# Block sums of the MLP's weights by adding transfers, and the MLP's pool opened ahead of the output projection

## The chip, the cores and the metric

The kernel runs on one core of a Trainium2 chip. The metric is device time in microseconds (us); before the change it was 2313.75 us, the median of three runs (2308.81 to 2314.91).

## The reference, cut to what matters

One residual block over 1024 tokens of width 1024, in float32:

```python
h = rms_norm(x, norm_mix_g)
q, k, v, conv_in, q_m, gate = split(h @ w_in)          # w_in: 1024 x 10240
y_attn = (diff_attention(q, k, v) normed) @ w_attn_o   # 8 heads, causal
y_conv = short_gated_conv(conv_in) @ w_conv_o
y_mem  = memory_attention(q_m, rms_norm(mem)) @ w_mem_o
merged = g0 * y_attn + g1 * y_conv + g2 * y_mem        # g = sigmoid(gate + b_gate)
x  = x + merged @ w_o                                  # the output projection
h2 = rms_norm(x, norm_mlp_g)
x  = x + relu(h2 @ w_mlp_in) ** 2 @ w_mlp_out          # the MLP, 1024 -> 4096 -> 1024
```

## The kernel before, in words

Every float32 matrix is split into a high part (a cast to fp32r on ACT) and a low part (raw minus high, on DVE or POOL), and every product is three matmuls: high by high, high by low, low by high. TensorE (PE) executes its instructions in the order in which the code issues them; the loads on the SP queue are pinned to one order too. DVE, ACT and POOL instructions are placed by a scheduler that respects the data and the buffers.

The program has five stages. (1) 0 to about 232 us: norm of x, keys, values and queries of the memory attention. (2) To about 1243 us: a loop of 64 attention passes (`for s in range(ns)`, L844 to L867; 8 heads by 8 row tiles). Between the steps of a pass, PE takes matmuls from a `stream` of independent products (conv inputs, gates). (3) The merge, to 1531.6 us: for the branches b = 2, 1, 0 (`branch_steps`), 8 column blocks each of the branch's output product. DVE multiplies it by its gate, POOL adds it to `merged`. In b = 0, ACT and DVE split `merged` at once into the tiles mT. (4) The output projection, to 1631.4 us: `w_o` in three column chunks (384, 384, 256), for each chunk 8 row tiles; 576 matmuls, 384 of them 384 wide, 192 of them 256 wide. DVE adds x, ACT squares, and in the last chunk `x2_norm(t)` scales the row tile (L885) and POOL issues its stores to `xn_dram` and `x2_dram`. (5) The MLP, in a new memory pool `xp`, whose tiles stand where the old pool's stood.

The MLP multiplies matrices of 2x2 blocks with seven block products (Strassen-Winograd) in place of eight. The up stage (`seq1`, `up(n)`) has 56 products of 24 matmuls each (8 column groups g by 7 products i), the down stage (`seq2`) 56 of 24 again. Four of the seven products need sums of weight blocks and four need sums of blocks of the normed rows. The weight sums are made by `sum_jobs` (w_mlp_in; 32 jobs: two SP loads of 256 KB into a tile `sumw`, four POOL operations of 128x256, one store of 512 KB issued by POOL), of which eight run in the attention loop (at `s % 8 == 6`) and the rest in the merge, and by `sum_jobs2` (w_mlp_out; 32 like jobs in the up stage). The rows come back from `xn_dram` into tiles `xr` (`load_rows`). `first_half(t)` transposes row tiles 0 to 3 on PE into X1 and X2 (`tps`, `put`: ACT casts the high part, DVE subtracts the low part). `second_sums(t)` makes the sums of rows t-4 and t (three POOL and one DVE subtraction into tiles tt and tu), and `second_half(t)` transposes them in three groups into X3 to X7, one t after each of the products up(0) to up(3). PSUM has two double banks named X and two named Z, which the transposes and the products share.

Of the kernel before, what the change touches and what calls it, by code (L numbers as in the profile page):

```python
# [60 lines left out]
def tile_hybrid_block(ctx: ExitStack, tc: tile.TileContext, x, mem, norm_mix_g, norm_mem_g, w_in, b_gate,  # L61
# [107 lines left out]

    def rstd_of(ss, n, width, tag):  # L170
# [3 lines left out]
        G.tensor_tensor(out=r, in0=r, in1=mhalf[:, 0:width], op=ALU.pow)  # L174
        return r
# [114 lines left out]
    sw1_dram = dram.tile([NG, P, 4, 4, 256], F32, name="sw1_dram")  # L290
    sw2_dram = dram.tile([NG, P, 4, 2, 512], F32, name="sw2_dram")
# [235 lines left out]
    def sub_(out, a, b):  # L527
        G.tensor_tensor(out=out, in0=a, in1=b, op=ALU.subtract)  # L528

    def sum_jobs():  # L530

        w1b = w_mlp_in.rearrange("(h k p) (c g n) -> h k p c g n", h=2, k=4, p=P, c=2, n=256)
        for g in range(NG):
            for k in range(4):
                z = rawt("sumw", (P, 2, 2, 256))
                for h in range(2):
                    load(z[:, h], w1b[h, k, :, :, g, :])
                a11, a21, a12, a22 = z[:, 0, 0], z[:, 0, 1], z[:, 1, 0], z[:, 1, 1]
                G.tensor_tensor(out=a22, in0=a21, in1=a22, op=ALU.add)  # L539
                sub_(a21, a11, a21)  # L540
                sub_(a11, a22, a11)
                sub_(a12, a12, a11)

                G.dma_start(sw1_dram[g, :, :, k, :], z.rearrange("p a b n -> p (a b) n"))
                yield

    def sum_jobs2(tile):
        w2b = w_mlp_out.rearrange("(h g j p) (d m n) -> h g j p d m n", h=2, j=2, p=P, d=2, n=256)
        for g in range(NG):
            for j in range(2):  # L550
                for m in range(2):
                    z = tile().rearrange("p a (b n) -> p a b n", b=2)
                    for h in range(2):
                        load(z[:, h], w2b[h, g, j, :, :, m, :])
                    b11, b12, b21, b22 = z[:, 0, 0], z[:, 0, 1], z[:, 1, 0], z[:, 1, 1]
                    sub_(b11, b12, b11)
                    sub_(b12, b22, b12)
                    sub_(b22, b22, b11)
                    sub_(b21, b21, b22)

                    G.dma_start(sw2_dram[g, :, :, j, m * 256:(m + 1) * 256], z.rearrange("p a b n -> p (a b) n"))
                    yield
# [4 lines left out]
    mT = ByChan()  # L567
# [23 lines left out]
    wos = [(0, 384, "wh"), (384, 384, "s"), (768, 256, "wh")]  # L591

    def load_wo(j):
        return load_w(w_o[:, wos[j][0]:wos[j][0] + wos[j][1]], wos[j][1], wos[j][2], V if j == 0 else None)

    def branch_steps(b):
        w_src = srcs[b][0]
        w, z = ready.pop(b)
        for c in range(KT):
# [3 lines left out]
            wn = load_w(w_src[:, (c + 1) * P:(c + 2) * P], P, "wh", V) if c + 1 < KT else None  # L603
            if b == 2:
                merged[c] = slot("merged", F32, tag="m")
            if c == KT - 1:
                if b:
                    prep(b - 1)
                else:
                    ready["wo"] = load_wo(0)  # L610
            if b == 0:
                mh, ml = mT.add("mT", ("fw" if c < 4 else "s", "m" if c else "s"))
            for hf in range(2):
# [3 lines left out]
                if hf:  # L617
                    run(jobs, 1)
# [221 lines left out]
    for s in range(ns):  # L840
# [24 lines left out]
        if s % 8 == 6:  # L865
# [348 lines left out]
```

## Time and profile before

The profiled execution took 2315.68 us; its span on the core is 2313.9 us.

| part of the span | us | PE busy | granted TensorE clock |
|---|---|---|---|
| whole | 2313.9 | 96% | 0.985 |
| attention loop, 300 to 1240 | 940.0 | 98% | 1.00 |
| merge, 1243 to 1531.6 | 288.6 | 97% | 0.98 |
| output projection, 1531.6 to 1631.4 | 99.8 | 94% | 0.95 |
| first MLP part, 1631.4 to 1740 | 108.6 | 70% | 0.81 |
| up stage, 1740 to 1940 | 200.0 | 100% | 1.00 |

Over the span DVE is busy 52%, ACT 41%, POOL 35%. PE's busy time is summed from records whose ends are modelled, so that a long row of matmuls is best timed by the starts of its first and last. A wait in a list names the engine or transfer whose end released the waiting instruction. A chain of waits goes backwards from the last instruction to what released it.

### The profile page before, as it was taken

Reading aid. Unit: us, or ns where it says so; the run is one execution under the profiler, and the core shown is the slowest. Engines: PE = TensorE matmul, PEld = TensorE weight load, DVE = VectorE, ACT = ScalarE, POOL = GpSimd, SP = SyncE. Lnnn points to the kernel's source line nnn. Section 1 sums busy time; section 2 is a strip of 40 time slices with the busy share of each in tenths; the row PEclk is TensorE's granted clock in tenths of the full one; section 3 lists DMA queues with packets and bytes.
Section 4 is the critical chain, followed back from the end, with each engine's and each line's share of the span. In section 5 each row is a group of like instructions: output and inputs, shape, how many; then the busy total and the mean of one; then the engine's idle time right before and its main releaser. Section 6 shows DMA issues by size and latency. Waiting matters only on the chain.

```text
span 2313.9 us, 31608 instructions
## 1 busy us (share of the span) xinstructions
PE 2219.8 (96%) x11472; PEld 1919.3 (83%) x11472; DVE 1213.6 (52%) x2200; ACT 953.1 (41%) x2190; POOL 811.6 (35%) x1084
## 2 busy tenths in 40 slices
PE   6999999999999999999999999989679999999999
PEld 6999888888888888888887887879568888788887
DVE  6755455555555555555556343342447676664452
ACT  5544445454545454444545232331222323354341
POOL 5422233333233232333334444641417788100000
PEclk9999999999999999999999999999789999999999
DMA  7412121222212121222214775752828999886660
GB/s 201 128 61 63 46 79 59 67 80 66 72 51 91 42 87 42 75 63 67 80 64 143 238 238 174 226 157 90 294 83 307 331 338 350 292 304 219 219 227 37
DMA packets 242748, 338.29 MB, mean 146 GB/s; under 512 B 20256, under 2 KB 182048, under 8 KB 242592
## 3 DMA queue, kind: packets, MB, share of 16 engines
q1 hardware_dynamic: 206128, 239.64, 32.5%
q0 software_dynamic: 19584, 71.31, 8.2%
q10 hardware_dynamic: 16880, 25.33, 3.1%
q8 instruction: 90, 1.47, 0.3%
q14 instruction: 66, 0.54, 0.1%
HBM read 235.56 MB, written 100.66 MB: 145 GB/s over the span
## 4 chain that ended last, share of the span: by engine, by line
PE 74%; DMA 10%; DVE 6%; POOL 4%; issue 3%; ACT 2%; SPq 1%; ACTq 0%; POOLq 0%; DVEq 0%
PE ps_mm L89 37%; PE X L89 14%; PE Z L89 11%; PE ps_sc L89 7%; DMA sumw<-in_w_mlp_in_dram 3%; PE ps_tr L93 3%; PE ps_tr L89 3%; POOL sumw L528 2%; DVE wlo L184 1%; DMA raw<-in_w_attn_o_dram 1%; DMA xr<-xn_dram 1%; SPq L98 1%; POOL merged L623 1%; DMA sw_dram<-sumw 1%; POOL sumw L539 1%
## 5 line engine op out<-in xcount | busy, mean ns | idle before, releaser
L89 PE MATMUL ps_mm<-hT,whi 128*128 128x512 f32 x1536 | 490.3, 400 | 1.7 <-DVE vst L668 1.7
L89 PEld LDWEIGHTS ps_mm<-hT,whi 128*128 128x128 f32 x1536 | 279.0, 189 | 53.3 <-DVE vst L668 4.7
L89 PE MATMUL ps_mm<-hT,wlo 128*128 128x512 f32 x768 | 301.7, 393 | 0.0
L89 PE MATMUL ps_mm<-whh,hT 128*128 128x384 f32 x1024 | 276.4, 340 | 1.9 <-DVE inner L475 1.9
L528 POOL TENSOR_TENSOR sumw<-sumw 128x256 f32<-128x256 f32 x224 | 215.0, 961 | 40.5 <-DMA sumw<-in_w_mlp_out_dram 29.6
L89 PEld LDWEIGHTS ps_mm<-whh,hT 128*128 128x128 f32 x1024 | 186.3, 188 | 7.2 <-DVE inner L475 3.7
L184 DVE TENSOR_TENSOR wlo<-raw,whi 128x256 fp32r<-128x256 f32 (+2 forms) x169 | 123.9, 749 | 121.4 <-ACT whi L202 108.6
L89 PE MATMUL X<-w,u 128*128 128x512 f32 x768 | 174.6, 389 | 0.0
L184 POOL TENSOR_TENSOR wlo<-raw,whi 128x512 fp32r<-128x512 f32 (+2 forms) x95 | 116.3, 1230 | 162.9 <-ACT whi L202 161.9
L89 PE MATMUL ps_mm<-whl,hT 128*128 128x384 f32 x512 | 171.4, 335 | 0.0
L89 PEld LDWEIGHTS X<-w,u 128*128 128x128 f32 x768 | 144.2, 188 | 29.9
L670 POOL TENSOR_TENSOR sq<-qk 128x256 f32<-128x256 f32 x64 | 42.6, 665 | 356.9 <-ACT qk L665 356.5
L89 PEld LDWEIGHTS ps_mm<-hT,wlo 128*128 128x128 f32 x768 | 144.7, 188 | 27.5
L202 ACT CAST whi<-raw 128x512 fp32r<-128x512 f32 (+2 forms) x264 | 127.0, 530 | 77.5 <-PE ps_mm L89 13.1
L174 POOL TENSOR_TENSOR r<-r,mhalf 128x1 f32<-128x1 f32 (+1 forms) x186 | 132.8, 714 | 14.4
L914 DVE TENSOR_TENSOR u<-uraw,u 128x1024 fp32r<-128x1024 f32 x56 | 72.1, 1288 | 118.9 <-ACT u L920 118.5
L89 PE MATMUL Z<-w,u 128*128 128x512 f32 x576 | 131.7, 390 | 1.6 <-DVE snap L917 1.6
L173 POOL TENSOR_SCALAR r<-ss 128x1 f32<-128x1 f32 (+1 forms) x186 | 39.7, 214 | 255.2 <-ACT ps_tr L764 106.0
L89 PEld LDWEIGHTS Z<-w,u 128*128 128x128 f32 x576 | 108.0, 188 | 24.8 <-DVE snap L917 2.4
L89 PE MATMUL ps_mm<-x,whi 128*128 128x512 f32 x384 | 120.6, 395 | 4.0 <-DVE x L184 3.3
L920 ACT CAST u<-uraw 128x1024 fp32r<-128x1024 f32 x56 | 59.0, 1054 | 156.9 <-PE X L89 74.6
L89 PE MATMUL ps_sc<-x,whi 128*128 128x512 f32 x384 | 118.8, 391 | 1.1 <-DVE gt L622 1.1
(236 smaller groups left out, 4836.1 us busy)
## 6 DMA issues: line engine op xcount, KB each, us to landing
sw_dram<-sumw POOLq DMA_DIRECT2D x64, 512.0 KB, 5.8
raw<-in_w_in_dram SPq DMA_DIRECT2D x56, 512.0 KB, 3.8
u_dram<-c POOLq DMA_DIRECT2D x56, 512.0 KB, 6.0
uraw<-u_dram SPq DMA_DIRECT2D x56, 512.0 KB, 5.3
sumw<-in_w_mlp_in_dram SPq DMA_DIRECT2D x64, 256.0 KB, 4.1
w1raw<-sw_dram SPq DMA_DIRECT2D x32, 512.0 KB, 6.6
sumw<-in_w_mlp_out_dram SPq DMA_DIRECT2D x64, 256.0 KB, 6.0
w2raw<-sw_dram SPq DMA_DIRECT2D x32, 512.0 KB, 4.3
```

The source lines that it names most:

```text
L89: return cls.pin(nc.tensor.matmul(*a, **kw))
L93: return cls.pin(nc.tensor.transpose(*a, **kw))
L98: return pin_load(nc.sync.dma_start(dst, src))
L173: G.tensor_scalar(r, ss, 1.0 / n, EPS, op0=ALU.mult, op1=ALU.add)
L174: G.tensor_tensor(out=r, in0=r, in1=mhalf[:, 0:width], op=ALU.pow)
L184: eng.tensor_tensor(out=lo, in0=raw, in1=f(hi), op=ALU.subtract)
L202: A.copy(out=hi[:, a:b, :], in_=raw[:, k0 + a:k0 + b, :])
L528: G.tensor_tensor(out=out, in0=a, in1=b, op=ALU.subtract)
L539: G.tensor_tensor(out=a22, in0=a21, in1=a22, op=ALU.add)
L670: G.tensor_tensor(out=sq, in0=qk, in1=qk, op=ALU.mult)
L914: eng.tensor_tensor(out=out, in0=a, in1=b, op=ALU.subtract)
L920: A.copy(out=hl[:, 0], in_=raw)
```

## The change

**Weight sums.** `sum_jobs` now issues 16 transfers from DRAM to DRAM on POOL's queue, eight for each weight, each of a quarter of a weight matrix (4.19 MB): eight plain copies and eight that add the source to what lies at the destination. A transfer that reads another one's result waits for it on POOL. One is issued at every third attention pass (`s % 3 == 1`, s = 1 to 46), behind the pass's last power operation of a norm. `sum_jobs2` and the `sumw` tiles are gone. Since the transfers only add, four operands have the opposite sign from before: `put` negates X4 and X5, and outputs are subtracted where they were added or squared after a minimum instead of a maximum. The loads of the sums read rows of 1 KB or 2 KB from the quarter matrices where they read one packed block.

**Merge and output projection.** In b = 0, POOL stores each half of `merged` to `mg_dram` (16 stores of 256 KB); the tiles mT are gone from the old pool. `old.close()` now stands ahead of the output projection. In the new pool, `load_m` brings `merged` back in pairs of column blocks and splits it, `load_wo` brings 8 full rows of blocks of w_o (512 KB) and splits them, `load_x` brings rows of x. The product is made in 512-wide halves, 384 matmuls in all: for t = 0 to 3 in four double banks at once, the column blocks k outside, 0 to 5 for all four, then the last two for each; then t = 4 to 7 one after the other.

**Rows of the MLP.** `wo_out` leaves the normed rows in SBUF (tiles xn, 7 buffers for 8 tiles); `xn_dram` is gone. `first_half(t - 4)` stands between the two halves of output tile t, `second_sums(t)` behind it, and the three groups of transposes of `second_half` stand between the matmuls of up(0) to up(3), eight matmuls apart. `seq1` begins with a list of 16 products. Some tiles change their pool slots (sn 4 to 3, c 6 to 7, halves for t, x's slots for the down stage's x2).

The diff, cut to its core:

```diff
+        last_norm[0] = G.tensor_tensor(out=r, in0=r, in1=mhalf[:, 0:width], op=ALU.pow)
...
+        def go(out, in_, op=ALU.bypass):
+            after(G.dma_start(out, in_, accum_op=op), last_norm[0])
+        a = [w_mlp_in[h * 512:(h + 1) * 512, c * 2048:(c + 1) * 2048] for c in range(2) for h in range(2)]
+        b = [w_mlp_out[h * 2048:(h + 1) * 2048, d * 512:(d + 1) * 512] for h in range(2) for d in range(2)]
+        for (q, t, r, s), z in ((a, sw1), ((b[0], b[2], b[1], b[3]), sw2)):
+            for i, src, op in ((0, r, 0), (1, r, 0), (0, s, 1), (1, q if z is sw1 else s, 1), (2, z[0 if z is sw1 else 1], 0),
+                               (2, q, 1), (3, z[2], 0), (3, t, 1)):
+                if z is sw2 and (i, op) == (0, 1):
+                    src = q
+                go(z[i], src, ALU.add if op else ALU.bypass)
                 yield
...
-            if b == 0:
-                mh, ml = mT.add("mT", ("fw" if c < 4 else "s", "m" if c else "s"))
...
-                    A.copy(out=mh[:, sl], in_=merged[c][:, sl])
-                    V.tensor_tensor(out=ml[:, sl], in0=merged[c][:, sl], in1=f(mh)[:, sl], op=ALU.subtract)
+                    G.dma_start(mg_dram[c][:, sl], merged[c][:, sl])
...
-        if s % 8 == 6:
+        if s % 3 == 1:
...
+    wo_op = [x8(f"wo{k}", (2, 1024)) for k in range(KT)]
+    m_op = {}
+    xn = {t: blk("xn", "c") for t in range(NT)}
+    m_op[1] = [x8("mT1", (2, 2, 512)) for _ in range(2)] + [wpair("mT1", 512) for _ in range(2)]
+    m_op[0] = [x8("mT0", (2, 2, 512)) for _ in range(4)]
+    tq = {t: half_blk("t2") for t in range(4, NT)}
+    xr = {}
+    def load_m(hf, kk):
+        r = raw4("mraw", 512)
+        load(r, mg_dram[2 * kk:2 * kk + 2, :, hf * 512:(hf + 1) * 512].rearrange("k p n -> p k n"))
+        split(m_op[hf][kk], r, V)
+    def load_wo(k):
+        r = raw4("woraw", 1024)
+        load(r, w_o[k * P:(k + 1) * P, :].rearrange("p (o n) -> p o n", o=1))
+        split(wo_op[k], r[:, 0, :], V)
+    def load_x(t):
+        xr[t] = blk("xr", "sn").rearrange("p h n -> p (h n)")
+        load(xr[t], x[t * P:(t + 1) * P, :])
...
+    def wo_out(t, ps):
+        x2 = xr.pop(t)
+        V.tensor_tensor(out=x2, in0=ps.rearrange("p h n -> p (h n)"), in1=x2, op=ALU.add)
+        ss = sm.tile([P, 1], F32, tag="ss1", bufs=3, name="ss")
+        xf = xn[t].rearrange("p h n -> p (h n)")
+        A.activation(xf, x2, AF.Square, accum_out=ss)
+        r = rstd_of(ss, D, 1, "r1")
+        V.scalar_tensor_tensor(out=xf, in0=x2, scalar=r, in1=g2_row, op0=ALU.mult, op1=ALU.mult)
+        G.dma_start(x2_dram[t], x2)
...
+    seq1 = [(0, 1), (0, 2), (1, 1), (1, 2), (0, 6), (0, 5), (0, 7), (1, 6), (0, 4), (1, 5), (0, 3), (1, 7), (2, 1),
+            (1, 4), (2, 2), (1, 3)]
...
-                load(r, sw1_dram[g, :, {6: 0, 7: 1, 3: 2, 5: 3}[i]])
+                load(r, sw1[{5: 0, 7: 1, 6: 2, 3: 3}[i]].rearrange("(k p) (g n) -> g p k n", p=P, n=256)[g])
...
+        if i in (4, 5):
+            A.activation(hi, src, AF.Copy, scale=-1.0)
+            V.scalar_tensor_tensor(out=lo, in0=src, scalar=-1.0, in1=f(hi), op0=ALU.mult, op1=ALU.subtract)
+        else:
+            A.copy(out=hi, in_=src)
+            sub(V, lo, src, f(hi))
...
+        ra, rb, n2 = xn[t - 4], xn[t], tq[t]
+        sub(G, ra[:, 0], rb[:, 0], ra[:, 0])
+        sub(V, rb[:, 0], rb[:, 1], rb[:, 0])
+        sub(G, n2, ra[:, 0], rb[:, 1])
+        add(G, ra[:, 1], ra[:, 1], n2)
...
+        ra, rb, n2 = xn.pop(t - 4), xn.pop(t), tq.pop(t)
+        for (i, a), (j, b) in (((3, rb[:, 1]), (7, rb[:, 0])), ((6, n2), (5, ra[:, 0])), ((4, ra[:, 1]), (0, None))):
             tp = tps(a, b, "Z")
             put(i, t, tp[:, 0])
             if j:
                 put(j, t, tp[:, 1])
+            yield
...
+                    if (12 * j + 3 * k + q) % 8 == 7 and k + j + q < 6:
+                        yield
...
+    load_m(0, 0)
+    load_wo(0)
+    load_wo(1)
+    for k in range(2, KT, 2):
+        load_m(0, k // 2)
+        load_wo(k)
+        load_wo(k + 1)
+        if k == 2:
+            load(g2_row, norm_mlp_g[0].unsqueeze(0).broadcast_to([P, D]))
+        if k >= 4:
+            for t in range(k - 4, k - 2) if k == 4 else (2,):
+                load_x(t)
+    load_m(1, 0)
+    load_m(1, 1)
+    load_x(3)
+    load_m(1, 2)
+    load_m(1, 3)
+    pss = [banks("XZ"[t % 2]) for t in range(4)]
+    for k in range(KT - 2):
+        for t in range(4):
+            wo_mm(pss[t], t, (k,))
     for t in range(4):
-        load_rows(t)
-    for n in range(4):
-        load1(n)
+        wo_mm(pss[t], t, (KT - 2, KT - 1))
+        wo_out(t, pss[t])
+        load_x(t + 4)
     alloc_x(1, 2)
...
+    for t in range(4, NT):
+        ps = banks("XZ"[t % 2])
+        wo_mm(ps, t, range(KT), (0,))
+        first_half(t - 4)
+        wo_mm(ps, t, range(KT), (1,))
+        wo_out(t, ps)
+        second_sums(t)
+        load1(t - 4)
+        if t >= 6:
+            split1(t - 6)
...
+            parts = second_half(4 + n)
+            for _ in up_steps(n):
+                run(parts, 1)
+            run(parts)
...
```

Three places where instructions stand otherwise. First PE where the merge ends and the output projection begins (ps_sc is the last branch product, mT and wo the projection's operands, X and Z the new pool's PSUM banks). Before:

```order
L89 MATMUL ps_sc<-x_14984,whi 128x512
L89 MATMUL ps_sc<-x_14985,whi 128x512
L89 MATMUL ps_sc<-x_14984,wlo 128x512
L89 MATMUL ps_mm<-whi,mT_15113 128x384
L89 MATMUL ps_mm<-wlo,mT_15113 128x384
L89 MATMUL ps_mm<-whi,mT_15114 128x384
L89 MATMUL ps_mm<-whi,mT_15198 128x384
L89 MATMUL ps_mm<-wlo,mT_15198 128x384
```

and with the change:

```order
L89 MATMUL ps_sc<-x_14823,whi 128x512
L89 MATMUL ps_sc<-x_14824,whi 128x512
L89 MATMUL ps_sc<-x_14823,wlo 128x512
L89 MATMUL X<-wo_15507,mT_15527 128x512 x6
L89 MATMUL Z<-wo_15507,mT_15527 128x512 x6
L89 MATMUL X<-wo_15507,mT_15527 128x512 x6
L89 MATMUL Z<-wo_15507,mT_15527 128x512 x6
L89 MATMUL X<-wo_15508,mT_15527 128x512 x6
```

The projection's matmuls go from 384 to 512 wide; a weight tile of `merged` meets both column halves of w_o, and the banks are the new pool's.

Second POOL in an attention pass with a sum job (r is a norm's power, sq and qd the queries' norm of the next pass, wlo a low part). Before:

```order
L173 TENSOR_SCALAR r<-ss 128x1
L174 TENSOR_TENSOR r<-r,mhalf 128x1
L184 TENSOR_TENSOR wlo<-raw,whi 128x512
L539 TENSOR_TENSOR sumw<-sumw 128x256
L670 TENSOR_TENSOR sq<-qk 128x256
L528 TENSOR_TENSOR sumw<-sumw 128x256
L173 TENSOR_SCALAR r<-ss_3891 128x4
L528 TENSOR_TENSOR sumw<-sumw 128x256
L174 TENSOR_TENSOR r<-r,mhalf 128x4
L528 TENSOR_TENSOR sumw<-sumw 128x256
L675 TENSOR_TENSOR qd<-qk,r 128x256
L544 DMA sw_dram<-sumw 512x1x256
```

and with the change:

```order
L175 TENSOR_SCALAR r<-ss 128x1
L176 TENSOR_TENSOR r<-r,mhalf 128x1
L532 DMA sw_90<-in_w_mlp_in_dram 512x2048
L186 TENSOR_TENSOR wlo<-raw,whi 128x512
L638 TENSOR_TENSOR sq<-qk 128x256
L175 TENSOR_SCALAR r<-ss_3749 128x4
L176 TENSOR_TENSOR r<-r,mhalf 128x4
```

The four operations on sumw and their store are gone, and one transfer stands behind the power operation, ahead of the low part and the next queries' squares.

Third PE around the end of the first up product (x1h and x1l are the transposed rows' parts, x2h and x2l the second's, ident the transposes' operand). Before:

```order
L89 MATMUL X<-x1l,w_16680 128x512
L89 MATMUL X<-x1h,w_16680 128x512
L93 MATMUL Z<-ident,xr 128x128 x4
L93 MATMUL Z<-ident,tu 128x128 x4
L93 MATMUL Z<-ident,tt 128x128 x8
L93 MATMUL Z<-ident,tu 128x128 x4
L89 MATMUL Z<-x2h,w_16735 128x512
L89 MATMUL Z<-x2l,w_16735 128x512
```

and with the change:

```order
L89 MATMUL X<-x1l,w_16077 128x512
L93 MATMUL Z<-ident,xn 128x128 x8
L89 MATMUL X<-x1h,w_16077 128x512 x2
L89 MATMUL X<-x1l,w_16077 128x512
L89 MATMUL X<-x1h,w_16077 128x512 x2
L89 MATMUL X<-x1l,w_16077 128x512
L89 MATMUL X<-x1h,w_16077 128x512 x2
L93 MATMUL Z<-ident,t_15531 128x128 x4
L93 MATMUL Z<-ident,xn 128x128 x4
L89 MATMUL X<-x1l,w_16077 128x512
L89 MATMUL X<-x1h,w_16077 128x512 x2
L89 MATMUL X<-x1l,w_16077 128x512
```

The transposes for X3 to X7, which stood in one row between two products, stand in groups of eight between matmuls of the product; their sources are the xn tiles and one half tile t in place of xr, tt and tu.

## Rows read from the trace of the kernel before

**Rows 1.** The page: busy in 40 slices of 57.8 us, tenths
```profile
PE   6999999999999999999999999989679999999999
```

**Rows 2.** PE's waits, 1540 to 1740: releaser, us in total, times, longest
```profile
PE Z L93 <- DVE x7l L914: 15.8, 4, 5.6
PE Z L93 <- DMA xr<-xn_dram: 8.6, 2, 5.7
```

**Rows 3.** Stretches: PE, PEld, DVE, ACT, POOL busy (instructions), clock, DMA, GB/s
```profile
300.00:1240.00 940.00, 923.88 (x4869) 805.84 (x4868) 509.90 (x1251) 453.82 (x1252) 309.52 (x465) 1.00 0.21 66
1243.00:1531.60 288.60, 279.41 (x1225) 228.46 (x1224) 119.83 (x190) 101.68 (x183) 142.25 (x159) 0.98 0.69 218
1531.60:1631.40 99.80, 93.32 (x577) 91.39 (x575) 31.91 (x55) 22.41 (x69) 29.15 (x41) 0.95 0.40 136
1631.40:1740.00 108.60, 76.54 (x323) 61.37 (x323) 48.46 (x55) 31.81 (x46) 24.29 (x24) 0.81 0.48 170
1640.00:1660.00 20.00, 14.92 (x56) 11.35 (x54) 9.20 (x12) 7.36 (x11) 1.20 (x1) 0.59 0.94 331
1740.00:1940.00 200.00, 200.00 (x884) 165.68 (x883) 139.46 (x96) 57.54 (x57) 163.63 (x177) 1.00 0.95 331
```

**Rows 4.** Chain of waits, 1595 to 1745: start, length, work
```profile
1628.88 7.76 DMA xn_dram<-xn
...
1638.49 8.28 DMA xr<-xn_dram
...
1652.61 6.06 DMA xr<-xn_dram
...
1718.54 5.44 PE Z L89 x24
```

**Rows 5.** PE's timeline, second output-projection product: start, length, operation, idle before
```profile
1542.92 0.69 PE L89 MATMUL ps_mm<-whi,mT 128*128 128x384 f32 x1 [3.63 <-ACT whi L202]
```

**Rows 6.** The page's groups: busy, mean ns of one, idle before, releaser
```profile
L914 DVE TENSOR_TENSOR u<-uraw,u 128x1024 fp32r<-128x1024 f32 x56 | 72.1, 1288 | 118.9 <-ACT u L920 118.5
...
L920 ACT CAST u<-uraw 128x1024 fp32r<-128x1024 f32 x56 | 59.0, 1054 | 156.9 <-PE X L89 74.6
```

**Rows 7.** Groups by shape, 1640 to 1740
```profile
L914 POOL TENSOR_TENSOR tt<-xr,tt 128x512 f32<-128x512 f32 x4 | 5.1, 1276 | 0.3
...
L93 PEld LDWEIGHTS Z<-ident,tt 128*128 128x128 f32 x32 | 3.5, 140 | 3.5 <-POOL tt L914 2.8 <-issue 0.7
```

**Rows 8.** Single lines: ns least, median, most; first and last start
```profile
L670 POOL TENSOR_TENSOR sq<-qk x64: 612/615/1062, 235.4 to 1240.1; 128x256 f32<-128x256 f32 x64
...
L544 POOL DMA_DIRECT2D sw_dram<-sumw x32: 715/728/881, 304.4 to 1539.8; - x32
...
L1034 POOL DMA_DIRECT2D u_dram<-c x56: 533/573/641, 1680.0 to 2015.0; - x56
```

**Rows 9.** POOL's timeline, one attention pass
```profile
637.68 0.61 POOL L670 TENSOR_TENSOR sq<-qk 128x256 f32<-128x256 f32 x1 [8.26 <-ACT qk L665]
```

**Rows 10.** DMA issues: queue, form, count, KB each, median us to landing
```profile
rawh<-in_w_in_dram SPq DMA_DIRECT2D x64, 192.0 KB, 2.8
...
gt<-z_dram SPq DMA_DIRECT2D x24, 512.0 KB, 5.0
w1raw<-in_w_mlp_in_dram SPq DMA_DIRECT2D x24, 512.0 KB, 8.0
...
o_dram<-osl ACTq DMA_DIRECT2D x16, 256.0 KB, 2.0
...
xn_dram<-xn POOLq DMA_DIRECT2D x8, 512.0 KB, 6.5
```

**Rows 11.** PE's waits in the merge, 1243 to 1531.6
```profile
PE ps_tr L93 <- DVE o L766: 3.9, 1, 3.9
```

**Rows 12.** PE's timeline where the up stage ends
```profile
1990.26 0.50 PE L89 MATMUL X<-x4h,w 128*128 128x512 f32 x1 [3.72 <-ACT snap L1053]
```

More of the change, by code (lines that the diff above doesn't have):

```diff
@@ L289, in tile_hybrid_block @@
     NG = DFF // 512
-    sw1_dram = dram.tile([NG, P, 4, 4, 256], F32, name="sw1_dram")
-    sw2_dram = dram.tile([NG, P, 4, 2, 512], F32, name="sw2_dram")
+    sw1 = [dram.tile([D // 2, DFF // 2], F32, name=f"sw1{i}") for i in range(4)]
+    sw2 = [dram.tile([DFF // 2, D // 2], F32, name=f"sw2{i}") for i in range(4)]
     memT = [[slot(f"memT{c}{kq}", shape=(P, 4, MEM)) for kq in range(2)] for c in "hl"]
@@ L547, in sum_jobs2 @@
[L547 to L562, printed above, removed]
+        def go(out, in_, op=ALU.bypass):
+            after(G.dma_start(out, in_, accum_op=op), last_norm[0])
@@ new lines, in tile_hybrid_block, with wo_mm @@
+    g2_row = xp.tile([P, S], F32, tag="g2", bufs=1, name="g2_row")
+    def wo_mm(ps, t, ks, hs=(0, 1)):
+        for h in hs:
+            for k in ks:
+                for a, b in ((0, 0), (0, 1), (1, 0)):
+                    T.matmul(ps[:, h, :], lhsT=m_op[t // 4][k // 2][:, a, k % 2, (t % 4) * P:(t % 4 + 1) * P],
+                             rhs=wo_op[k][:, b, h * 512:(h + 1) * 512], start=k == 0 and a + b == 0,
+                             stop=k == KT - 1 and a == 1, skip_group_check=True)
@@ L978, in put @@
         hi, lo = (z[:, :, (t % 4) * P:(t % 4 + 1) * P] for z in X[i])
-        A.copy(out=hi, in_=src)
-        sub(V, lo, src, f(hi))
-    rows = {}
-    def load_rows(t):
-        r = rows[t] = blk("xr", "sn")
-        load(r.rearrange("p h n -> p (h n)"), xn_dram[t])
+        if i in (4, 5):
[4 more added lines that the diff above has]
+            sub(V, lo, src, f(hi))
     def tps(a, b, key):
@@ L1038, in up, with up_steps @@
     def up(n):
+        run(up_steps(n))
+    def up_steps(n):
         g, i = seq1[n]
@@ L1065, in up @@
             c11, c12, c21, c22 = (B.pop((g, c)) for c in ("c11", "c12", "c21", "c22"))
-            add(V, c22, c12, c22)
+            sub(V, c22, c22, c12)
             sub(V, c12, c11, c12)
-            sub(V, c11, c22, c11)
-            sub(V, c21, c21, c11)
+            V.scalar_tensor_tensor(out=c11, in0=c22, scalar=-1.0, in1=c11, op0=ALU.mult, op1=ALU.subtract)
+            V.scalar_tensor_tensor(out=c21, in0=c21, scalar=-1.0, in1=c11, op0=ALU.mult, op1=ALU.subtract)
             for k, t in ((5, c22), (7, c12), (6, c11), (3, c21)):
                 put_u(k, g, t)
+    load_m(0, 0)
[19 more added lines that the diff above has]
+            wo_mm(pss[t], t, (k,))
     for t in range(4):
-        load_rows(t)
-    for n in range(4):
-        load1(n)
+        wo_mm(pss[t], t, (KT - 2, KT - 1))
+        wo_out(t, pss[t])
+        load_x(t + 4)
     alloc_x(1, 2)
-    split1(0)
-    for t in range(4):
-        first_half(t)
-    split1(1)
+    for t in range(4, NT):
[8 more added lines that the diff above has]
+            split1(t - 6)
     alloc_x(6, 5, 7, 4, 3)
-    jobs = sum_jobs2(lambda: blk("sumw", "t"))
     for n in range(len(seq1)):
-        if 9 < n < 48 and n % 7 != 3:
-            run(jobs, 1)
         load1(n + 4)
```

123 lines of the change are left out of this document (35 added, 88 removed).

## The prediction

> **What bounds the kernel now.** I read the slices of the page first, to see where TensorE (PE) isn't the bound; then the stretches, which give each stage its own busy times; then, in the weak stages, PE's waits and the chain of waits; and last the mean durations of the operations that the change adds or moves. The slices show PE at nine tenths or more except in four: the first (6), the one around the merge's end (8), and the two that hold the output projection's end and the MLP's first part (6 and 7) [rows 1]. The stretches say the same in numbers: attention leaves 940.0 - 923.9 = 16.1 us without PE, the merge 288.6 - 279.4 = 9.2, the output projection 6.5, the MLP's first part 32.1 of 108.6, and the up stage none [rows 3]. So what the change does to POOL's load in the attention, the merge and the up stage can be worth at most those gaps, while the MLP's first part is worth looking into. There PE waits 15.8 us in four waits for the last low part of the transposed rows (x7l, on DVE) and 8.6 us for two loads of the rows from DRAM [rows 2], and its clock is at 0.81 of full speed in the mean, 0.59 in its worst 20 us, that is between the two levels of 1.2 and 2.4 GHz [rows 3]. The chain shows why: the last row tile's store takes 7.76 us, its load 8.28, the next load 6.06, and only then can sums, transposes and splits follow one another [rows 4].
>
> **The change part by part.** All terms are for the profiled execution, 2315.68 us.
>
> *A, the output projection.* Before: 99.8 us [rows 3]. After: 384 matmuls 512 wide; a row of 24 such took 5.44 us, 0.2267 each [rows 4], so 87.1 us. That is -12.7. Part of it is only that waits inside the stage, such as the 3.63 us ahead of the second product [rows 5], are not counted in the new one, so the new one's own must be added. The pool's boundary makes one: `merged` no longer goes from DVE straight to PE but through DRAM. The first `load_m` stands on SP behind the last branch's stores of the earlier column blocks and takes its buffer from the old pool, so I let it start some 4 us before the last branch product ends (a half column block, 24 matmuls, is 5.4 us of PE; an addition of this shape on POOL takes 1.28 of it [rows 7]). Then come a load of `merged` and one of w_o (5.0 us for a 512 KB load from DRAM, and an estimated 1.5 for the second at the 331 GB/s that the core reached [rows 3, 10]), a cast of 1.05 and a subtraction of 1.29 [rows 6], partly one beside another: 4 us early against about 9 us of work is a hole of 5. Its bounds are 1 (the second load hidden, only casts left) and 10 (nothing starts before the branch ends). Later column blocks hide: a pair needs 1.5 MB, 4.8 us at 331 GB/s, three casts (3.2 us) and three subtractions (3.9), beside 48 matmuls or 10.9 us of PE. The last `merged` blocks are wanted 6 x 24 matmuls (32.6 us) after the first, more than their addition, store (2.0 for a 256 KB store on another queue), load and split together. After a hole, the clock may be low: 2 us, bounds 0 and 4 (twice the time for some 4 us of matmuls). A = -12.7 + 5 + 2 = **-5.7** (-11.7 to +1.3).
>
> *B, the MLP's first part.* Of the 108.6 us, the work that stays is 211 of the 24-row matmuls at 0.2267, 47.8 us, and 112 transposes at 0.140 (their weight loads, which pace them) [rows 4, 7], 15.7: together 63.5. The other 45.1 are the waits [rows 2], smaller ones, and the low clock. With the rows left in SBUF, the store and load in the chain go; first_half's transposes have half an output product (24 matmuls, 5.4 us) ahead of their tile's next use; and the 28 transposes of second_half have eight matmuls (1.8 us) between groups, in which ACT's cast (0.59) and DVE's subtraction (0.69) of one 512-wide part can run. What is late next: (1) at t = 4, whose operand comes through `load_m(1, ...)`, which SP holds behind `load_x(3)`, which waits for a free buffer, hence for tile 0's normed row and its store; I take 2.5 us, bounds 0 (the store is done within the following three tiles' 8 us) and 8 (xr's load of 8.28 [rows 4] in full). (2) In up(0) to up(3) DVE does per product five low parts (3.4 us), one sum (0.7), one weight split (1.3) and its outputs (two or three of 1.2), some 8 to 9 us, beside 24 matmuls and 28 transposes, 9.4 us: close to even, so a group of transposes can wait for the Z bank; 4 us in four products, bounds 0 and 16 (the 15.8 us of now, unchanged [rows 2]). (3) The clock: 1, bounds 0 and 4. B = -45.1 + 7.5 = **-37.6** (-45.1 to -17.1).
>
> *C, the up and down stages.* PE is busy 200 of 200 us there with 163.6 us of POOL work and 331 GB/s of transfers beside it [rows 3]; taking `sum_jobs2` out of it gives PE nothing. The wait of 3.72 us at the end of the up stage [rows 12] has the same two products next to each other after the change, so I leave it: **0** (-3.7 to 0). The loads of the sums in shorter rows (1 and 2 KB) are issued four products, 22 us, ahead, against 8.0 us of the slowest kind of weight load [rows 10].
>
> *D, the merge.* 24 of the 32 sum jobs leave it: POOL's four operations each, 24 issues of 0.73 [rows 8], and 48 loads on SP. POOL gets 16 stores (0.57 each [rows 8]) and half of the weights' low parts. Of the 9.2 us that PE idles, 3.9 wait for an output of the attention's last pass [rows 11], which is not touched. **-2** (-4 to +3, the upper end being a store that holds POOL's addition up).
>
> *E, attention with 16 transfers.* A pass takes (1240.1 - 235.4) / 63 = 15.95 us [rows 8], three of them 47.8. A plain copy reads and writes 4.19 MB, 8.4 MB: 25 us at 331 GB/s; one that adds reads twice, 12.6 MB: 38 us; with the 21% that the loop's own transfers take [rows 3], 48. POOL's issue costs it up to 0.73 us for 512 pieces [rows 8], an estimated 2 for the longest here, and POOL has a gap of 8.26 us in each pass [rows 9]; so neither issue nor, at these durations, the waits of one transfer for another reach PE. Bounds of a copy: 12 us, if 331 GB/s holds in each direction by itself, and 64 us, if it goes no faster than one w_mlp_in load (512 KB in 8.0 us, 65.5 GB/s [rows 10]); I take 25 to 38 as nearest to a row that shows the engines full. The eight old jobs in the loop save a little POOL time. **+2** (-3 to +30 by rival 3; rival 1 lies beyond). The Trainium skill, "DMA: Bandwidth & Descriptors", section "Latency and other measured facts", has DRAM-to-DRAM copies at 207 to 214 GB/s in each direction: by it a copy would take an estimated 20 us; "Collectives: The Full Stack", section on the bandwidth ceiling, says that an add needs two source reads and so runs at half the rate: an estimated 40 us. No row here shows either; by both the sum would be the same.
>
> Sum: -5.7 - 37.6 + 0 - 2 + 2 = -43.3, 2315.68 - 43.3 = 2272.4. The profiled execution stands 1.9 us above the median of the runs; taken off, **2270 us**.
>
> **The rivals.** *1, slower: the transfers don't keep up.* POOL executes in order, and a transfer that waits for another one's landing holds behind it the norm's power, the next queries' squares and qd, for which PE's transposes of the next pass wait. A weight needs four copies and four additions, 10c if an addition takes 1.5c, in eight places of 47.8 us, 382 us. From c = 38 us (110 GB/s) on, PE pays the rest; with c = 45 it is 2 x (450 - 382) = 136 us: 2406. The gain is eaten at 2 x (10c - 382) = 43.3, c = 40.4, an addition of 60.6 us or 69 GB/s. For it: the 65.5 GB/s row, and that no transfer of the trace adds. Against: that row is a single transfer's time from issue to landing among others, and the same engines moved 331 GB/s together. Chance 0.10.
>
> *2, half the gain stays away: the new boundary and the first products are fed one after another.* All of the hole (10), the stall at t = 4 (8) and the products' wait for DVE (16) come: +22.5 against the forecast, 2293. For it: every operand passes SP, ACT and DVE in one order, and DVE's load in up(0) to up(3) is near PE's. Against: these are three bounds at once. Chance 0.14.
>
> *3, the transfers slow the loop's own loads.* A head's weights take 2.8 us per load at the loop's 66 GB/s [rows 3, 10]; if a load beside a 4 MB transfer takes the 8.0 us of w1raw [rows 10], eight heads lose 8 x 5.2 = 42 us, of which some 38 of each 47.8 us have a transfer under way: about 30 in place of 2, 2298. The Trainium skill's DMA page, section "Issuing engines are not separate DMA queues", has transfers of all issuers interleave on the same 16 engines, which is this rival's mechanism. For it: in the merge at 218 GB/s PE loses 3% of its time, in the loop at 66 GB/s 1.7% [rows 3]. Against: at 331 GB/s the up stage lost nothing [rows 3], its loads being issued early. Chance 0.09.
>
> **How the numbers follow.** The forecast holds 0.67; within it the bounds of A and B alone, not all at one end, give about 2254 to 2286. For 8 in 10 the range takes in rivals 2 and 3 and some of the lower bounds: 2246 to 2302; left out are rival 1 and what lies below. A measurement of this kernel can tell about 0.3%, 7 us, from no change. Faster by more: all of the forecast and rivals 2 and 3 but for mishaps that add up, 0.87; within: 0.03; slower: rival 1, 0.10.
>
> **What would show it right or wrong.** A: from the first matmul on wo to the last, less the transposes, under 100 us, with one hole of about 5 us at its start. B: no store and load of rows in the chain, PE's waits in the first four up products together under 10 us, and a clock above 0.9 where it was 0.81. D: the merge within 4 us of now. E: an attention pass still at 16 us, additions landing within 48 us of their issue, and no wait of POOL's queue for them that PE's next transposes inherit. C: the up stage's 200 us as they are. It is wrong if passes with a transfer are longer than those without (rivals 1 or 3), or if the time from the merge's end to the up stage's full rate shrinks by less than 25 us (rival 2).

## The result and the profile after

The changed kernel takes 2261.15 us in the median of four runs (2257.83 to 2262.22), against 2313.48 before in the same comparison: a ratio of 0.9775, 95% interval 0.9758 to 0.9792, or 52.3 us. The forecast was 2270, with a range of 2246 to 2302. The profiled execution took 2260.93 us, its span 2259.2, 54.7 less than before.

The slices of the changed kernel, which answer to [rows 1]: the weak places at the merge's end and at the MLP's beginning are gone from view.

```profile
PE   6999999999999999999999999999999999999999
```

The stretches (columns as in [rows 3]: from and to, length, busy time of PE, PEld, DVE, ACT, POOL with their instructions, granted clock, DMA share, GB/s) of the changed kernel: attention, merge, output projection with the first transposes, the first four up products, and the rest of the up stage.

```profile
300.00:1229.00 929.00, 921.45 (x4866) 807.66 (x4865) 509.92 (x1250) 452.52 (x1251) 297.54 (x438) 1.00 0.47 126
1232.00:1511.60 279.60, 275.80 (x1225) 227.27 (x1223) 97.81 (x143) 94.01 (x166) 98.32 (x94) 0.99 0.47 151
1512.00:1616.80 104.80, 97.49 (x417) 79.07 (x418) 46.87 (x44) 29.54 (x39) 25.28 (x32) 0.93 0.49 175
1616.80:1662.00 45.20, 35.45 (x179) 28.26 (x179) 25.53 (x31) 19.10 (x29) 7.19 (x7) 0.92 0.25 82
1662.00:1946.60 284.60, 282.64 (x1247) 233.74 (x1246) 157.21 (x134) 87.29 (x89) 27.19 (x51) 1.00 0.57 198
```

The stages are best timed by marks that both kernels have: the first and the last `sq` on POOL (one per pass), the end of the merge's matmuls, and the first down product. The line of `sq` after, which answers to the first of [rows 8]:

```profile
L638 POOL TENSOR_TENSOR sq<-qk x64: 605/615/1062, 234.7 to 1229.2; 128x256 f32<-128x256 f32 x64
```

From such rows, in us:

| stage | before | only the transfers | after | forecast of the step |
|---|---|---|---|---|
| to the first sq | 235.4 | 235.4 | 234.7 | |
| first to last sq (attention) | 1004.7 | 994.4 | 994.5 | E: +2 |
| last sq to the merge's end | 291.5 | 283.7 | 282.5 | D: -2 |
| merge's end to the first down product | 471.3 | 458.5 | 434.9 | A, B and C: -43.3 |
| from there to the end | 311.0 | 311.1 | 312.6 | |

The middle column is an experiment, below. The forecast's sum of 43.3 was 11.4 us short of these 54.7 (9 us between the medians); its terms were off by more: the gain in the projection and the first products was sized 7 us too large, and the attention and the merge, for which I saw next to nothing, gave 19 of the 54.7.

### The profile page after: what moved, and what is told of

Its sections match the earlier page's. It is cut to its first block, busy times and chain, and to the rows that moved or that the text cites. A ratio compares the mean times of both kernels' runs of the same rounds, so it can differ in the third digit from the quotient of the medians.

```text
span 2259.2 us, 30413 instructions
## 1 busy us (share of the span) xinstructions
PE 2200.5 (97%) x11280; PEld 1893.7 (84%) x11280; DVE 1165.6 (52%) x2127; ACT 943.8 (42%) x2134; POOL 574.3 (25%) x813
## 3 DMA queue, kind: packets, MB, share of 16 engines
q1 hardware_dynamic: 183760, 203.98, 27.6%
## 4 chain that ended last, share of the span: by engine, by line
PE 89%; DVE 4%; DMA 3%; ACT 2%; issue 2%; POOL 0%; SPq 0%; ACTq 0%; DVEq 0%; POOLq 0%
PE ps_mm L89 42%; PE X L89 16%; PE Z L89 13%; PE ps_sc L89 11%; PE ps_tr L89 3%; PE ps_tr L93 3%; DVE wlo L186 1%; PE Z L93 1%; DMA rawh<-in_w_in_dram 0%; DVE ql L666 0%; ACT qh L661 0%; DMA w2raw<-in_w_mlp_out_dram 0%; DMA mraw<-mg_dram 0%; DMA xt<-in_x_dram 0%; DVE whl L186 0%
## 5 line engine op out<-in xcount | busy, mean ns | idle before, releaser
L186 POOL TENSOR_TENSOR wlo<-raw,whi 128x512 fp32r<-128x512 f32 (+2 forms) x120 | 139.1, 1164 | 214.0 <-ACT whi L204 186.5
L89 PEld LDWEIGHTS X<-w,u 128*128 128x128 f32 x768 | 144.1, 188 | 31.6 <-ACT snap L1185 1.7
L89 PEld LDWEIGHTS ps_mm<-hT,wlo 128*128 128x128 f32 x768 | 144.9, 189 | 27.6
L204 ACT CAST whi<-raw 128x512 fp32r<-128x512 f32 (+2 forms) x240 | 117.8, 537 | 66.7 <-PE ps_sc L89 22.0
L186 DVE TENSOR_TENSOR wlo<-raw,whi 128x512 fp32r<-128x512 f32 (+2 forms) x120 | 102.4, 857 | 68.9 <-ACT whi L204 68.2
L691 ACT ACTIVATE e<-ps_sc,negm 128x256 f32<-128x256 f32 (+7 forms) x128 | 94.1, 740 | 31.6 <-DVE negm L688 31.6
L1020 POOL DMA_DIRECT2D u_dram<-c x56 | 29.9, 535 | 300.7 <-DVE c L1016 148.9
L89 PE MATMUL ps_mm<-whi,hT 128*128 128x256 f32 x512 | 102.9, 292 | 0.0
```

Of the source, the lines that this page charges most:

```text
L89: return cls.pin(nc.tensor.matmul(*a, **kw))
L186: eng.tensor_tensor(out=lo, in0=raw, in1=f(hi), op=ALU.subtract)
L204: A.copy(out=hi[:, a:b, :], in_=raw[:, k0 + a:k0 + b, :])
L691: A.activation(e[:, 0:n], sc[:, 0:n], AF.Exp, scale=-1.0, bias=negm[:, c:c + 1], accum_out=sums[:, c:c + 1])
L1020: G.dma_start(u_dram[i, g], t)
```

## The experiments

Medians, and ratios to the kernel before in the same comparison (2314.6 to 2315.4 us) with their 95% intervals.

**The sums left out, in the kernel before.**

```diff
-    jobs = sum_jobs()
+    jobs = iter(())                 # likewise sum_jobs2
-                load(r, sw1_dram[g, ...])
+                load(r, w1v[0, 0, g])   # likewise w_mlp_out's
```

> The kernel before with the weight sums left out: the products that need a sum load a plain weight block in its place, so the output is not the reference's. Theory 1 (the old sum jobs cost TensorE time: in the loop because their POOL operations stand ahead of qd, in the merge by their loads and POOL work): the loop shortens by about 10 us (first to last sq 1004.7 to about 994.5, and PE's eight waits for qd, 7.3 us, are gone), the merge by about 7 (291.5 to about 284 from the last sq), the rest unchanged; some 2297. Theory 2 (the loop and the merge got shorter through other edits: where weight splits run, merged not split in the merge): less than 3 us in either, 2309 or more.

Measured: 2281.26 us, 0.9857 (0.9843 to 0.9870), that is 34 us, twice what I expected. `sq` runs from 236.3 to 1228.1: 991.8 us. The merge takes 282.4, the stretch to the first down product 457.2.

```profile
L670 POOL TENSOR_TENSOR sq<-qk x64: 612/613/1062, 236.3 to 1228.1; 128x256 f32<-128x256 f32 x64
```

Theory 2 is out. The 14 us in the stretch to the first down product were not expected: the output projection alone went from 99.5 to 89.5 us between its first and last matmul (mT), in the kernel before and in this one:

```profile
L89 PE MATMUL ps_mm<-whi,mT x384: 278/334/687, 1531.6 to 1631.1; 128*128 128x384 f32 x128, 128*128 128x256 f32 x64
L89 PE MATMUL ps_mm<-whi,mT x384: 278/334/346, 1510.5 to 1600.0; 128*128 128x384 f32 x128, 128*128 128x256 f32 x64
```

What the old jobs did is seen in PE's waits of the attention in the kernel before (releaser, us in total, times, longest), a row that the prediction doesn't use:

```profile
PE ps_tr L93 <- POOL qd L675: 7.3, 8, 1.0
```

Without the sums PE has no wait for qd. POOL's timeline shows a pass with a job (start, length, operation), and last the qd of the pass without one in [rows 9]. From sq's start to qd's it takes 4.05 us with the job, 2.53 without.

```profile
299.78 0.61 POOL L670 TENSOR_TENSOR sq<-qk 128x256 f32<-128x256 f32 x1
300.35 0.74 POOL L528 TENSOR_TENSOR sumw<-sumw 128x256 f32<-128x256 f32 x1
301.18 0.20 POOL L173 TENSOR_SCALAR r<-ss 128x4 f32<-128x4 f32 x1
301.46 0.73 POOL L528 TENSOR_TENSOR sumw<-sumw 128x256 f32<-128x256 f32 x1
302.15 1.02 POOL L174 TENSOR_TENSOR r<-r,mhalf 128x4 f32<-128x4 f32 x1
303.14 0.73 POOL L528 TENSOR_TENSOR sumw<-sumw 128x256 f32<-128x256 f32 x1
303.83 0.61 POOL L675 TENSOR_TENSOR qd<-qk,r 128x256 f32<-128x256 f32 x1
...
640.21 1.02 POOL L675 TENSOR_TENSOR qd<-qk,r 128x256 f32<-128x256 f32 x1
```

The scheduler had filled the chain sq, power, qd with the job's subtractions, one in each gap, rather than the long gap after it. qd comes 1.5 us later in these two, and PE waits for it 0.8 to 1.0 us: eight jobs, eight waits. These 7.3 us are the larger part of what the loop lost; the rest I can't name. At the merge's end the chain of waits in the kernel before runs through the same operations, ahead of POOL's additions to `merged` on which the projection's operand hangs:

```profile
1514.19 0.93 POOL sumw L528
...
1515.18 0.86 POOL sumw L528
...
1516.05 1.26 POOL merged L623
...
1517.75 4.90 DMA raw<-in_w_o_dram
...
1525.66 1.30 POOL merged L623
...
1530.03 3.63 DMA sumw<-in_w_mlp_in_dram
```

**Only the transfers, in the kernel before.** The change's `sum_jobs`, one job at `s % 3 == 1`, `sum_jobs2` gone, the loads of sums as in the change; merge, projection and MLP as before.

> The kernel before with only the first part of the change: the 16 transfers in place of both kinds of sum jobs, everything else as before. The changes of sign in the MLP are not carried over, so the output is not the reference's. Theory 1, with transfers that cost nothing: as the kernel without sums, about 2297 (within 3 us of it). Theory 3 (the transfers cost the loop time by contention or by POOL's waits): more than 5 us above the kernel without sums, in the loop. Theory 2: 2309 or more.

Measured: 2286.87 us, 0.9879 (0.9865 to 0.9892): 28.5 us of the change's 52.3. The attention takes 994.4 us, 2.6 more than without any sums, the merge 1.3 more, the stretch behind it 1.3 more; the total of 5.6 is at the edge of theory 3, but half of it isn't in the loop.

```profile
L648 POOL TENSOR_TENSOR sq<-qk x64: 603/613/1063, 235.4 to 1229.8; 128x256 f32<-128x256 f32 x64
```

The cause of the 5.6 us is open. The loop's 2.6 are no more than single profiles differ by: eight kernels whose loop is the changed kernel's own show 993.5 to 997.2 us. So a little over half of the gain is the first part of the change by itself.

**The changed kernel without its transfers.**

```diff
-    jobs = sum_jobs()
+    jobs = iter(())     # and plain weight blocks loaded in place of the sums
```

> The changed kernel with the 16 transfers left out; the products that need a sum load a plain weight block, so the output is not the reference's. Theory 1: the loop as now (994.5 from first to last sq, within 2 us) and 2261 in all, within 3. Theory 3: the loop more than 5 us shorter.

Measured: 2261.17 us, 0.9770 (0.9757 to 0.9784), and 994.5 us from first to last sq. As they are spaced, the transfers cost nothing that can be measured in the whole. A trace of them is in PE's waits of the loop: for the low part of a head's weights (whl) they sum to 2.5 us in the changed kernel and 2.6 in the one with only the transfers, and there are none in the kernels without transfers.

**A transfer in every pass, and in every second.**

```diff
-        if s % 3 == 1:
+        if s >= 1:          # the other: if s % 2 == 1:
```

> The changed kernel with one transfer in each of the first 16 passes from s = 1 in place of every third pass. Rival 1 of the prediction by its mechanism: a weight's four copies and four additions, about 20 and 30 us each as they landed, need some 200 us where eight passes give 128, POOL waits for a named transfer some 35 to 45 us per weight ahead of the norms, of which a gap of 8 us per pass hides part: the loop 25 to 45 us longer, 2286 to 2306. If POOL's waits are hidden or the transfers overlap freely: the same as the changed kernel, 2261 within 3.

Measured: 2340.46 us, 1.0109 (1.0091 to 1.0127): slower than before the change. The loop takes 1071.9 us, 77 more, where I expected 25 to 45. POOL did wait for named transfers, 28.8 us in five waits, less than the 70 to 90 that I expected:

```profile
POOL sw L532 <- DMA sw<-in_w_mlp_out_dram: 18.8, 1, 18.8
POOL sw L532 <- DMA sw<-sw: 10.0, 4, 5.8
```

But PE's long waits are for ACT: 27.2 us for evictions of PSUM banks (z) and 26.5 for casts of a head's weights (whh). The stretches from 270 to 620 show the engines of the transfers full and PE's clock down, the one after them neither:

```profile
270.00:340.00 70.00, 55.52 (x291) 48.14 (x289) 29.74 (x75) 24.63 (x71) 20.00 (x31) 0.92 0.92 246
340.00:440.00 100.00, 79.66 (x399) 69.71 (x400) 41.52 (x100) 39.07 (x107) 27.98 (x42) 0.87 0.83 217
440.00:620.00 180.00, 149.92 (x734) 130.39 (x733) 79.08 (x193) 67.97 (x189) 52.80 (x73) 0.90 1.01 243
620.00:700.00 80.00, 79.58 (x424) 69.57 (x423) 46.56 (x106) 41.61 (x108) 25.88 (x38) 1.00 0.24 76
```

and the chain of waits there goes through a head's weights:

```profile
319.19 21.45 DMA rawh<-in_w_in_dram
```

> The changed kernel with a transfer at every second pass, 31.6 us apart. Copies landed in 15 to 19 us, additions in 24 to 32 at every third pass. If the loop is hurt only where two transfers overlap (at every pass additions took up to 43 us, a head's weight loads 21): the loop within 3 us of 994.5, 2261 to 2264. If each transfer costs the loads beside it something: the loop 8 to 25 us longer, 2270 to 2286.

Measured: 2304.73 us, 0.9952 (0.9938 to 0.9965), above both forecasts; the loop 1037.7 us, 43 more, with only one wait of POOL for a transfer, 1.0 us. Here it is seen how a head's weights hold PE. ACT's timeline (start, length, operation, idle before and its releaser):

```profile
468.93 0.51 ACT L612 CAST whh<-rawh 128x384 fp32r<-128x384 f32 x1 [9.81 <-DMA rawh<-in_w_in_dram]
469.46 0.59 ACT L502 COPY z<-ps_mm 128x512 f32<-128x512 f32 x1
```

and PE's beside it:

```profile
470.10 0.69 PE L89 MATMUL ps_mm<-whh,hT 128*128 128x384 f32 x1 [7.55 <-ACT z L502]
```

The cast is for the next head, whose weights PE doesn't need yet. But ACT executes in order, behind the cast stands the eviction z, and PE waits for z's PSUM bank. The load was issued at 456.2, some 3 us ahead of the cast's place in the queue, enough for the 2.8 us of [rows 10], and landed 12.7 us later, while an addition issued at 442.3 was under way. There are four such waits of PE of 5.5 to 8.8 us, each with an addition under way (issued at 339.1, 442.3, 614.6 and 718.4), and the clock is low behind them (0.74 in the 20 us from 460). In the changed kernel the first loads of the heads go out at 317.9, 442.6, 569.6, 695.5, 821.2 and 947.5, and the transfers beside them begin 2 us later (319.8, 697.4), have landed (at 439.4), or land within 2.5 us (571.3, 823.6, 948.5): ACT's waits for these weights sum to 11.4 us, the longest 2.0, where they are 45.4 here.

```profile
ACT whh L612 <- DMA rawh<-in_w_in_dram: 45.4, 17, 9.8
ACT whh L612 <- DMA rawh<-in_w_in_dram: 11.4, 15, 2.0
```

It is the additions that hold the loads: where a head's loads meet a plain copy, ACT's longest wait is 2.9 us here (loads from 595.5, a copy from 581.6 to 600.4) and 2.0 in the changed kernel (loads from 947.5, a copy until 948.5). So it is rival 3 that becomes slow, not rival 1, and the change escapes it since its heads' loads meet copies, or only the last 2.5 us of an addition: by a few us of phase, which no run has shifted by itself.

**Transposes in a row.**

```diff
-            for _ in up_steps(n):
-                run(parts, 1)
-            run(parts)
+            up(n)
+            run(parts)
```

> The changed kernel with second_half's transposes in one row behind each of the first four up products, as before, in place of between their matmuls. Theory 4 (the gain of the pool's part comes from the rows that stay in SBUF and from the interleaving in like shares; before, PE waited 15.8 us for x7l in the same places): about 10 us slower than the changed kernel, 2271, with waits for x7l of 10 us or more back. Theory 5 (the rows in SBUF alone give the gain, and DVE's and ACT's own queues bound the first products in either order): within 3 us, 2261.

Measured: 2273.46 us, 0.9824 (0.9807 to 0.9842): 12 us slower than the changed kernel, theory 4. PE's waits from the first up product on:

```profile
PE Z L93 <- DVE x7l L854: 14.4, 4, 4.5
```

That is the wait of [rows 2], back nearly whole: keeping the rows in SBUF doesn't remove it, the interleaving does. From the kernel with only the transfers (2286.87 us) to this one it is 13 us, from this one to the changed kernel 12; how the 13 divide between the projection and the rows in SBUF no run shows.

**The order of the loads ahead of t = 4.**

```diff
-    load_x(3)
     load_m(1, 2)
     load_m(1, 3)
+    load_x(3)
```

> The changed kernel with the load of x's row tile 3 behind the loads of merged for t = 4 to 7 in place of ahead of its last two. Prediction's step: that load waits for a buffer freed by tile 0, the two loads of merged stand behind it on SP, and PE loses 7.5 us at t = 4 (4.0 of waits, the rest low clock). If so: the loads of merged go out some 25 us earlier, no wait at t = 4, 5 to 8 us faster, 2254. Rival: the loads of merged wait for their own buffers (freed by splits) just as long: within 2 us.

Measured: 2256.10 us, 0.9750 (0.9735 to 0.9764), 5 us faster than the changed kernel. SP's timeline of the changed kernel, then of this one (start, length, loads, their number):

```profile
1529.19 4.29 SPq L98 DMA_DIRECT2D mraw<-mg_dram  x2
1559.00 0.35 SPq L98 DMA_DIRECT2D xr<-in_x_dram  x1
1559.44 1.47 SPq L98 DMA_DIRECT2D mraw<-mg_dram  x2
```

```profile
1532.02 6.84 SPq L98 DMA_DIRECT2D mraw<-mg_dram  x4
1561.41 0.34 SPq L98 DMA_DIRECT2D xr<-in_x_dram  x1
```

The last two loads of merged had stood 25 us behind x's row tile. PE's waits for mT at t = 4 are gone, and the time from the first projection matmul to the first up product falls from 104.5 to 96.3 us.

**Three smaller edits.** w_o's first two loads ahead of merged's:

```diff
-    load_m(0, 0)
     load_wo(0)
     load_wo(1)
+    load_m(0, 0)
```

> The changed kernel with the first two loads of w_o ahead of the first load of merged. In the changed kernel PE waits 3.6 us at the pool's boundary and loses 6.8 with the low clock; the wait is for the low part of w_o's first block on DVE. If the order of loads and splits sets that hole: 2 to 4 us faster, 2258. Rival: SP's first load of either kind waits for the old pool's last reader, and the hole only moves to merged's parts: within 2 us.

2262.54 us, 0.9771: no change. The hole moves from w_o's low part to merged's, as its rival said.

The second group of transposes of up(0) and up(1) in bank X:

```diff
-            tp = tps(a, b, "Z")
+            tp = tps(a, b, "X" if t < 6 and i == 6 else "Z")
```

> The changed kernel with the second group of transposes of up(0) and up(1) in the free double bank X in place of Z. In the trace of the changed kernel the first products and their transposes lose 14 us: 3.7 in one wait of up(1) for x5l, which frees the Z bank it needs, the rest in waits of about 1 us for Z and in the low clock behind them. Theory 6 (the two Z banks are what is short): up(1) no longer waits for x5l, 3 to 6 us faster, 2256. Theory 5 (DVE and ACT, which make the low and high parts in one queue with weight splits and snapshots, are what is short): within 2 us.

2259.43 us, 0.9761: 1.7 us, within the spread, as theory 5 has it. The waits move from x5l to x4l (3.3 us).

x5 ahead of the snapshot and of the next weight block (cut; H and L hold put's casts and subtractions):

```diff
+            ch = A.copy(out=t[:, 0], in_=r)
+            c = V.tensor_tensor(out=t[:, 1], in0=r, in1=f(t)[:, 0], op=ALU.subtract)
+            if n in (3, 5):
+                after(ch, H[5, n + 1])
+                after(c, L[5, n + 1])
...
-            A.copy(out=s, in_=ps)
+            c = A.copy(out=s, in_=ps)
+            if n in (0, 2):
+                after(c, H[5, 4 + n])
```

> The changed kernel with one order pinned in the first up products: ACT casts x5h ahead of the snapshot of up(0) and the cast of the next weight block, and DVE makes x5l ahead of that block's low part (likewise two products later). Theory 5 (the order of ACT's and DVE's queues holds PE there): the wait of 3.7 us of up(1) for x5l goes, with the low clock behind it 4 to 7 us faster than the changed kernel, 2256. Rival (the wait moves on to the next group's x3l and x7l): within 2 us, 2261.

2260.62 us, 0.9766 (0.9753 to 0.9780): not told apart from the changed kernel in the whole, which is what the rival said. In the stretch from the projection's first matmul to the first down product its profile gained 5 us (434.5 to 429.4), 3 of them in the first four up products; its attention was 2.7 longer, which is within the 993.5 to 997.2 us of kernels with this loop. The rival was near: of PE's waits in the first up products x5l falls from 4.3 to 2.1 us, x4l rises from 0.8 to 2.2:

```profile
PE Z L93 <- DVE c L857: 2.8, 2, 1.4
PE Z L93 <- DVE x4l L977: 2.2, 2, 1.4
PE Z L89 <- DVE x5l L977: 2.1, 2, 1.5
PE Z L93 <- DVE x7l L854: 2.0, 2, 1.0
```

**Both orders, and both with the bank.** The edits of x's row tile and of x5 together, then the bank's too.

> Both changes of order together: x's row tile 3 loaded behind merged's parts (alone 5.1 us in the median, 10.3 in the stretch from the projection to the down stage) and x5 first. If the two holes are independent: the sum of both alone, 2248 to 2252. If one hides the other: no better than the better one alone, about 2256.

2253.41 us, 0.9736 (0.9722 to 0.9749), between its two cases and faster than the changed kernel beyond both intervals; against the load's order alone (2256.10) the 2.7 us are within them, so what x5 adds is not shown in the whole.

> As the run with both orders, and the second group of transposes of up(0) and up(1) in the free bank X. Alone the bank gave 1.8 us, within the spread. Theory 6 (the banks are short once the queues are in order): 2 to 4 us faster than without it, 2247. Theory 5: within 2 us of it.

2252.12 us, 0.9735 (0.9721 to 0.9750): theory 5, the bank adds nothing to be measured. These two are the fastest versions, some 8 to 9 us ahead of the change and 61 to 63 ahead of the kernel before.

## Why the prediction was right, and where its terms were not

The direction and the size were right, and two of the mechanisms (the hole at the boundary, the rows left in SBUF with interleaved transposes); that the sum came close is luck, since errors of both signs met.

*E, attention, forecast +2, measured -10.2.* The failed step is "The eight old jobs in the loop save a little POOL time", which rested on POOL's gap of 8.26 us per pass [rows 9]. A gap is no proof that work is put in it: the job's operations stood in the short gaps of the chain to qd, and PE's own wait list of the loop, which I did not read since PE is at 98% there, named it with 7.3 us. That the transfers cost next to nothing held, and they landed sooner than my values: copies landed in 15.0 to 19.1 us and additions in 24.1 to 31.6, where I had 25 and 38.

*D, merge, forecast -2, measured -9.0.* "Of the 9.2 us that PE idles" was taken as the limit of the gain, but the clock was part of it too. In the stretches, PE's idle time fell from 9.2 to 3.8 us, and its busy time for the same 1225 instructions from 279.4 to 275.8. With only the transfers the merge is 7.8 shorter, so nearly all of it is the sum jobs'.

*A, forecast -5.7.* The sum charged the old stage's 99.8 us against new matmuls of 87.1, as though the old waits belonged to the old way of computing. Ten of the 12.7 us belong to the sum jobs: without them the old projection takes 89.5. The new one takes 104.5 us to the first up product, and 101.0 without its 32 transposes (0.11 each: the tiles t = 5 to 7 take 35.3 us for 144 matmuls and 24 transposes). So by itself, the stall at t = 4 included, it is no gain, and what the pool's earlier opening brings lies in B. The new hole is as forecast: PE's waits at the boundary are 3.6 us, and the first 24 matmuls end 12.3 us after the merge's last, 6.8 more than they need (forecast 5 + 2), at a mean granted clock of 0.71:

```profile
PE X L89 <- ACT mT L860: 3.5, 2, 2.3
PE X L89 <- DVE wo L854: 3.1, 1, 3.1
```

The first of these rows is t = 4: that stall was named with its cause, SP's order behind `load_x(3)`, and sized at 2.5 us of 0 to 8. With the low clock behind it (0.82 in the mean of the tile), it is 7.7 (19.5 us for 48 matmuls and 8 transposes that need 11.8), and the run with the other order shows that it was the order.

*B, forecast -37.6.* The mechanism held: store and load are gone, the waits of [rows 2] for x7l fall from 15.8 to 1.8 us, and the run with the transposes in a row brings 14.4 us of them back. Its size did not: 4 us were set for the first four up products, and they lose 14 (44.7 us for 96 matmuls, 21.8, and 80 transposes at 0.11, 8.8). I had counted 28 transposes for each product where there are 20, so PE's side looked as long as DVE's 8 to 9 us, and it is 7.6. PE's waits there sum to 9.7 us, and the longest, of 3.7 us, is that of up(1) for x5l:

```profile
1628.29 0.76 PE L89 MATMUL Z<-x2h,w 128*128 128x512 f32 x1 [3.73 <-DVE x5l L970]
```

In the 6 us behind it the granted clock is 0.51, the lower level. In the profile with x5 first the waits' sum falls only to 9.1 us, but none is over 1.5, the clock of the stretch is 1.00 in place of 0.92, and the matmuls and transposes take 2.5 us less.

Together, the stretch of A, B and C measured -36.4: -12.8 by the transfers alone and -23.6 by the pool and the rows.

*C, forecast 0.* PE stays at its rate in the up stage as forecast, and its last wait is 2.0 us (3.72 before [rows 12]).

*The rivals.* Rival 2 did come in part: two of its three bounds were nearly met (the stall 7.7 of 8, the products 14 of 16), and it was hidden by what the sums gave. Rival 3 is real and avoided by the spacing. Rival 1's wait was seen at length only at three times the density, where rival 3 costs more.

*The signs.* Of those named, A's failed (101.0 us where under 100 was named), and D's (9.0 us where within 4 was named). B's held (waits of 9.7 us, clock 0.92), C's, and E's (a pass takes (1229.2 - 234.7) / 63 = 15.8 us, additions land within 31.6).

The Trainium skill's pages gave an estimated 20 us for a copy and 40 for an addition ("DMA: Bandwidth & Descriptors", section "Latency and other measured facts"; "Collectives: The Full Stack", section "The bandwidth ceiling: the fold count and why AG ≠ RS ≠ AR"). The first page's figures are of copies issued by the sync and scalar queues, at the row pitches that reach the full rate; the second's half rate is that of a ring of cores. Here a copy beside the loop's loads moved 4.19 MB in 15.0 to 19.1 us, 220 to 280 GB/s in each direction, above the page's 207 to 214; an addition took 24.1 to 31.6, about 1.65 of a copy and not twice. The measurements decide. The Trainium skill's rule that transfers of all issuers share the same engines ("DMA: Bandwidth & Descriptors", section "Issuing engines are not separate DMA queues") agrees: a head's load took 12.7 us beside an addition, 2.8 in the median of the kernel before.

## What to carry to other kernels

Read the wait list of the stage in which the main engine is busiest as well: eight waits of 0.9 us don't show in a busy share of 98%, and helper work on a side engine is paid for where the scheduler puts it in a chain, not where the engine has room. Before crediting a new scheme with the old stage's waits, ask whose waits they are; a kernel with one part left out tells it in a single run. Large background transfers are next to free or cost 40 us by whether they meet the few loads on which an engine's queue is about to wait, so place them by those loads and not by their mean bandwidth.

## What the runs showed of the hardware

A DRAM-to-DRAM transfer of 4.19 MB that adds took only about 1.65 times a plain copy's time (24.1 to 31.6 us against 15.0 to 19.1). Its issue cost POOL 1.1 us in rows of 8 KB (w_mlp_in) and 1.9 in rows of 2 KB (w_mlp_out), where it also landed later (27.6 to 31.6 us against 24.1 to 26.0).

Behind one wait of 3.7 us of TensorE the granted clock was 0.51 for 6 us, and the matmuls and transposes there took 2.8 us more than at the full clock. In the run with x5 first, where the waits of the same stretch sum to nearly as much (9.1 us against 9.7) and none is over 1.5, the clock stayed at 1.00.

Contention between transfers showed first in the latency of small loads: a load of 192 KB took 12.7 us beside one addition and 21.5 with a transfer in every pass, where the kernel before has 2.8 in the median.
